# Experts with at most 64 rows: whole fp32 products in two column halves, weights in 8 KB runs, another order of the experts

## The chip, the cores and the metric

The program runs on one core of a Trainium2 chip, in one launch. Its time is the device time of that core in microseconds, the median of three runs. A separate execution was profiled; the rows below come from it.

## The reference, cut to what matters

The reference is one encoder block over 1024 + 512 tokens of width 1024: a projection, a pooling mixer, differential attention, an output projection, and a mixture of experts. The change touches the experts alone:

```python
hid = jax.nn.silu(xblk @ w_gate[e]) * (xblk @ w_up[e])    # 1024 -> 512, twice
y   = hid @ w_down[e]                                     # 512 -> 1024
# 32 experts; each token goes to 2 of them, its rows are gated and summed back
```

All of it is fp32. The three weights of an expert are 6 MB, so the 32 experts read about 200 MB whatever their rows are; a row (a token sent to an expert) costs a gather of 4 KB before and an adding scatter of 4 KB behind.

## The kernel before, in words

After attention and routing, `experts()` goes through a plan of 32 slots. The first two slots are fixed experts; the other 30 are filled at run time with the experts sorted by their number of rows, and each slot has a capacity in rows (`CAPS`, from 256 down to 32). `ORDER` says in which order the slots are worked off. Thirteen slots have a capacity of 64 or 32; this text calls them light, and the other seventeen plus the two fixed ones' rows heavy.

A slot is cut into blocks of at most 128 rows. For slot i, TensorE does gate(i), up(i) and then down(i-1), the down product of the slot before. Between the products stand transposes (L1109): those of the next slot's rows and those of the hidden values.

An fp32 product is not taken whole on this path. `split` (called from `use`, seven half-pieces ahead) writes a rounded copy `ew_hi` of the weights on ScalarE (L103) and the remainder `ew_lo` on VectorE (L107), both fp32r, and the rows get the same two parts. A block with more than 64 rows takes three fp32r products per 128 x 512 piece of weight (L111 to L113). A block of up to 64 rows has its high and low rows side by side as up to 128 columns of the stationary operand, and takes two (L1093, L1094); `both` adds the two halves of the result afterwards. In nine light slots, marked 4 in `NATIVE`, the down product is taken whole from the raw weights in fp32 (L1071), with the block's 64 or 32 columns as stationary operand; a whole product stands in the trace as two passes.

The raw weights come in pieces of 1 MB (`er_raw`, eight buffers), issued by SyncE in the order of their use (L1041), two pieces for each of gate, up and down. A buffer is free again when its split is done, or where the product is whole, when TensorE has read it. GpSimd issues the gathers (L1133, two slots ahead) and the adding scatters (L1179); each scatter waits for the one before it to land. The last two slots, 29 and 28, are not scattered before the end: their results are stacked and added by one matmul per half tile (L1207) to the sums that are read back from memory (`er_raw<-acc`, L1333, after the last scatter), and the final norm follows.

```python
NATIVE = (0,) * 17 + (4, 0, 4, 4, 4, 4, 0, 4, 0, 4, 4, 0, 4) + (0,) * STATIC
CAPS = (256,) * 2 + (224,) * 2 + (192,) + (160,) * 3 + (128,) * 4 + (96,) * 5 + (64,) * 9 + (32,) * 4 + (160, 128)
```

Of the kernel before, what the change touches and what calls it, by code (L numbers as in the profile page):

```python
# [10 lines left out]
F32 = mybir.dt.float32  # L11
F32R = mybir.dt.float32r
# [31 lines left out]
IDS = 4  # L44
AROWS = 64
PACE = (3, 1, 1, 1, 1, 1, 1, 0)
NATIVE = (0,) * 17 + (4, 0, 4, 4, 4, 4, 0, 4, 0, 4, 4, 0, 4) + (0,) * STATIC
DELAY = dict(out=1, hidden=1, silu=1, evac=1, turn_h=2, turn_x=4, end_h=3, stack=3)
ORDER = (11, 7, 26, 20, 23, 1, 24, 25, 14, 2, 21, 8, 3, 19, 18, 9, 4, 16, 5, 15, 0, 27, 22, 12, 13, 6, 17, 10, 29, 28)
CAPS = (256,) * 2 + (224,) * 2 + (192,) + (160,) * 3 + (128,) * 4 + (96,) * 5 + (64,) * 9 + (32,) * 4 + (160, 128)  # L50
VORDER = tuple(range(8, 12)) + tuple(range(8))
TGORDER = (2, 0, 1)
# [518 lines left out]
def layout(i):  # L571
    f = lambda n: np.asarray(i[n])
    a = {}
    x = np.concatenate([f("x_prompt")[0], f("x_sample")[0]], 0)
    a["x"] = x
    a["xT"] = x.T
    a["g_mix"] = f("g_mix")[0].reshape(8, 128).T
    a["pool_scale"] = f("pool_scale")[0].reshape(4, 128).T
    a["subln_g"] = f("subln_g")[0].reshape(128, 1)
    a["w_pool"] = f("w_pool")[0]  # L580
    for n in ("lambda_q1", "lambda_k1", "lambda_q2", "lambda_k2"):
        a[n] = f(n)[0]
    w = f("w_in")[0]
    pieces = []

    def piece(cols):
        n = cols.shape[1]
        k = cols.shape[0] // 128
        pieces.append(cols.reshape(k, 128, n).transpose(1, 0, 2).reshape(128, k * n))

    for g in range(2):
        piece(w[:, g * 256:(g + 1) * 256])
    for g in range(2):
        for o in (512, 1024):
# [12 lines left out]
    a["w_router"] = wr  # L607
    br = np.full((1, 40), -1e30, np.float32)
    br[0, :NE] = f("b_router_expert")[0]
    br[0, NE:NE + 4] = f("b_router_group")[0]  # L610
    a["b_router"] = br
    for n in ("w_gate", "w_up", "w_down"):
        a[n] = f(n)[0]
    return a


# [380 lines left out]
    nc.vector.scalar_tensor_tensor(K["ovs"], row[:1, :MAXOV], 128.0, st[:1], op0=OP.mult, op1=OP.add)  # L997


def natives(count):  # L1000

    return range(4) if count == 4 else range(1, 1 + count)


class Experts:
    def __init__(self, tc, A, S, K):
        self.tc, self.nc, self.A, self.S, self.K = tc, tc.nc, A, S, K
# [27 lines left out]
    def fetch(self, name, ev, i, queue=None):  # L1035
        n = D if name == "w_down" else FF
        k = 2048 // n
        raw = self.raw()
        w = self.A[name][ev:ev + 1] if isinstance(ev, int) else self.A[name][ds(ev, 1)]
        src = w.rearrange("o (k p) n -> p (o k) n", p=128)[:, i * k:(i + 1) * k]  # L1040
        (queue or self.nc.sync).dma_start(raw.rearrange("p (k n) -> p k n", k=k), src)  # L1041
        return raw, k

    def split(self, piece, h):
# [5 lines left out]
        split_lo(self.nc, lo, raw[:, s], hi)  # L1050
        return hi.rearrange("p (k n) -> p k n", k=k // 2), lo.rearrange("p (k n) -> p k n", k=k // 2)

    def ids(self, start, m, native=0, early=False):
# [3 lines left out]
        for p in range(0, 2 * m if m <= 64 else m, m):  # L1057
            nc.sync.dma_start(ix[p:p + m], src)
        return Block(self, m, ix, native, early, src)

    def proj(self, blocks, ps, w, i):
        for k in range(2):
            for b, p in zip(blocks, ps):
                b.mm(p, b.x, i * 2 + k, w[0][:, k], w[1][:, k], i + k == 0, i * 2 + k == 7)

    def down(self, blocks, ps, w, i):
        for b, (p0, p1) in zip(blocks, ps):
            for hf, p in enumerate((p0, p1)):
                s = slice(hf * 512, (hf + 1) * 512)
                if i in natives(b.native):  # L1070
                    self.nc.tensor.matmul(p[:b.m], lhsT=b.h[:, 0, i, :b.m].bitcast(F32), rhs=w[:, s], start=i == 0,  # L1071
                                          stop=i == 3)
                else:
                    b.mm(p, b.h, i, w[0][:, 0, s], w[1][:, 0, s], i == 0, i == 3)

    def bank(self):
        return self.PM([128, 512], F32, "m")
# [2 lines left out]
class Block:  # L1080


    def __init__(self, E, m, ix, native=0, early=False, src=None):
        self.native, self.early, self.src = native, early, src
        self.side = m <= 64
        self.E, self.nc, self.m, self.ix = E, E.nc, m, ix
        self.id = E.K["ident"]
        self.gate = ix[:, 1:2].bitcast(F32)

    def mm(self, p, x, k, wh, wl, first, last):  # L1090
        m = self.m
# [6 lines left out]
    def turn(self, out, src, n, pool=None):  # L1098

        nc, m = self.nc, self.m  # L1100
        per = min(4 if m > 64 else 8, n)

        def step(k0):
            p = []

            def fill():
                p.append((pool or self.E.PT)([128, per, m], F32, "t"))
                for k in range(per):
                    nc.tensor.transpose(p[0][:, k], src[:m, (k0 + k) * 128:(k0 + k + 1) * 128], self.id[:m, :m])  # L1109

            def empty():
                nat = natives(self.native) if n == 4 else range(0)
                if nat:
                    ks = slice(nat.start, nat.stop)
                    nc.scalar.activation(out[:, 0, ks, :m].bitcast(F32), p[0][:, ks], AF.Copy)
                for a, z in ((0, nat.start), (nat.stop, per)) if nat else ((0, per),):
                    if a == z:
                        continue
                    ks = slice(k0 + a, k0 + z)
                    hi = out[:, 0, ks, :m]  # L1120
                    lo = out[:, 0, ks, m:2 * m] if self.side else out[:, 1, ks, :m]
                    nc.scalar.activation(hi, p[0][:, a:z], AF.Copy)  # L1122
                    nc.vector.tensor_tensor(lo, p[0][:, a:z], hi.bitcast(F32), OP.subtract)  # L1123

            return fill, empty

        return [step(k0) for k0 in range(0, n, per)]
# [8 lines left out]
    def turn_x(self, pool=None):  # L1136
        if self.early:
            self.x = self.E.rows().bitcast(F32R).rearrange("p (o k m) -> p o k m", o=1, k=8)
        else:
            self.x = self.E.X([128, 2, 8, 128], F32R, "x", bufs=4)  # L1140
        return self.turn(self.x, self.xg, 8, pool)

    def turn_h(self):
        self.h = self.E.X([128, 2, 4, 128], F32R, "h", bufs=2)
        return self.turn(self.h, self.s, 4)

    def both(self, p, tag):
        nc, m = self.nc, self.m
        t = self.E.X([64, 512], F32, tag, bufs=1)[:m]
        nc.scalar.activation(t, p[m:2 * m], AF.Copy)  # L1150
        nc.vector.tensor_tensor(t, t, p[:m], OP.add)
        return t

# [13 lines left out]
    def weigh(self, ps):  # L1167
        nc, m = self.nc, self.m
        self.y = y = self.E.X([128, D], F32, "y")
        for hf, p in enumerate(ps):  # L1170
            d = y[:m, hf * 512:(hf + 1) * 512]
            if self.native == 4 or not self.side:
# [91 lines left out]
def experts(tc, A, S, K, RO, outs):  # L1264
    nc = tc.nc
    E = Experts(tc, A, S, K)
    with ExitStack() as ctx:
# [5 lines left out]
        def expert(i):  # L1273
# [4 lines left out]
                ev[i] = e  # L1278
            return ev[i]

        def ids(i):
            if i >= n:
                return
# [3 lines left out]
                o = AROWS  # L1287
            while o < cap:
                m = min(128, cap - o)
                bl.append(E.ids(expert(i) * ES + o, m, NATIVE[plan[i][0]]))  # L1290
                o += m
            blocks[i] = bl
            if i == n - 1:
# [51 lines left out]
        def split(k):  # L1345
            while at[1] < min(k, len(parts)):
                j = at[1] // 2
                fetch(j + 1)
                name, i, h, l = parts[at[1]]
                if name == "w_down" and h * 2 + l in natives(NATIVE[plan[i][0]]):  # L1350
                    pieces[parts[at[1]]] = raws[j][0][:, l * 1024:(l + 1) * 1024]
                else:
                    pieces[parts[at[1]]] = E.split(raws[j], l)
# [67 lines left out]
        for i in range(n + 1):  # L1421
# [24 lines left out]
            if i == n - 1:  # L1446
                after(DELAY["end_h"], lambda: turn(blocks[n - 1][0].turn_h()))
            if i:
                pd = [(E.bank(), E.bank()) for _ in blocks[i - 1]]
# [106 lines left out]
```

## Time and profile before

| what | us |
|---|---|
| median of 3 runs (1453.98 to 1455.87) | 1455.33 |
| the profiled execution | 1458.79 |
| its span, first to last instruction | 1456.5 |

The experts start at about 716 us of the span and their last product ends near 1401 us. Busy times are those of an engine, transfers are shown as the share of the 16 DMA engines, and a chain is the list of what released what, read from the end backwards. Matmul rows overlap their successors, so the distance between two starts, not the duration, is what one costs.

### The profile page before, as it was taken

To read this page: it belongs to the slowest core of one execution; us is meant where nothing else is said; L and a number is where in the kernel's file an instruction comes from. 1 tells how busy PE (TensorE), PEld (TensorE's weight loads), DVE (VectorE), ACT (ScalarE), POOL (GpSimd) and SP (SyncE) were. 2 spreads that over 40 slices of the span, in tenths; PEclk is the share of its full clock that TensorE was granted. 3 is DMA by queue.
4 is the path that set the end of the run, shared out by engine and by line. 5 is a ranking of instruction groups with operands and counts; after the bars stand their busy time and mean duration, and the time that the engine had idled before them with its cause. 6 is when DMAs were issued, how large, how long until landed. Compare 5 with 4: busy or idle time off the path is not lost.

```text
span 1456.5 us, 18022 instructions
## 1 busy us (share of the span) xinstructions
PE 1352.4 (93%) x5986; PEld 985.0 (68%) x5986; DVE 980.2 (67%) x1508; ACT 789.7 (54%) x1159; POOL 256.6 (18%) x376
## 2 busy tenths in 40 slices
PE   7899999987999999998599999999999999999970
PEld 5768888855667667876367757676767777667630
DVE  5486552085988637564677876877688786778774
ACT  6321112175887623221367776866587675777761
POOL 0000000003332210221211231322122221210132
PEclk9999999998999999999799999999999999999985
DMA  8535325066650057313699999999999997999874
GB/s 295 208 123 200 138 87 144 29 153 136 154 136 30 29 192 257 117 46 106 224 374 313 335 330 367 325 366 319 337 348 375 343 318 248 335 354 361 301 265 163
DMA packets 147694, 337.96 MB, mean 232 GB/s; under 512 B 17616, under 2 KB 25296, under 8 KB 147600
## 3 DMA queue, kind: packets, MB, share of 16 engines
q1 hardware_dynamic: 136688, 302.95, 60.0%
q0 software_dynamic: 9312, 29.65, 8.6%
q10 hardware_dynamic: 1600, 4.19, 0.8%
q8 instruction: 48, 0.79, 0.2%
q14 instruction: 46, 0.38, 0.1%
HBM read 282.69 MB, written 54.06 MB: 231 GB/s over the span
## 4 chain that ended last, share of the span: by engine, by line
PE 82%; DVE 6%; DMA 5%; ACT 2%; POOL 2%; issue 2%; SPq 0%; POOLq 0%; DVEq 0%; ACTq 0%
PE pm_m L111 9%; PE pm_m L113 9%; PE pm_m L112 9%; PE pm_m L1093 5%; PE pz_z L112 5%; PE pz_z L113 5%; PE pz_z L111 5%; PE pm_m L1094 5%; PE ps_sc L385 5%; PE po_o L443 4%; PE pm_m L1071 4%; PE pt_t L1109 3%; PE ph_h L112 2%; PE ph_h L111 2%; PE ph_h L113 2%; PE pt_t L430 2%
## 5 line engine op out<-in xcount | busy, mean ns | idle before, releaser
L107 DVE TENSOR_TENSOR ew_lo<-er_raw,ew_hi 128x1024 fp32r<-128x1024 f32 x348 | 413.1, 1218 | 113.3 <-ACT ew_hi L103 111.8
L103 ACT ACTIVATE ew_hi<-er_raw 128x1024 fp32r<-128x1024 f32 x348 | 354.9, 1052 | 55.5 <-PE pm_m L113 42.4
L111 PE MATMUL pm_m<-ew_hi,ex_x 128*128 128x512 f32 (+1 forms) x368 | 148.9, 405 | 0.2 <-ACT ex_x L1122 0.2
L113 PE MATMUL pm_m<-ew_hi,ex_x 128*128 128x512 f32 (+1 forms) x368 | 145.7, 396 | 0.2 <-DVE ex_x L1123 0.2
L112 PE MATMUL pm_m<-ew_lo,ex_x 128*128 128x512 f32 (+1 forms) x368 | 145.7, 396 | 0.0
L1179 POOL DMA_INDIRECT acc<-ex_y,ex_ix x40 | 90.4, 2260 | 251.3 <-ACT ex_y L1173 151.4
L111 PE MATMUL pz_z<-xT_hi,w_hi 128*128 128x512 f32 x288 | 114.8, 400 | 8.3 <-ACT xT_hi L152 8.3
L112 PE MATMUL pz_z<-xT_lo,w_hi 128*128 128x512 f32 x288 | 114.9, 399 | 0.0
L113 PE MATMUL pz_z<-xT_hi,w_lo 128*128 128x512 f32 x288 | 113.3, 393 | 0.0
L385 PE MATMUL ps_sc<-st_st 128*128 128x512 f32 x320 | 99.6, 452 | 11.5 <-ACT sm_e L404 5.6
L1093 PE MATMUL pm_m<-ew_hi,ex_x 128*128 128x512 f32 (+1 forms) x272 | 109.1, 401 | 0.0
L1094 PE MATMUL pm_m<-ew_lo,ex_x 128*128 128x512 f32 (+1 forms) x272 | 107.7, 396 | 0.1
L400 ACT ACTIVATE sm_e<-ps_sc,sb_m 128x1024 f32<-128x1024 f32 x64 | 70.8, 1111 | 45.6 <-PE pt_t L430 44.2
L389 DVE TENSOR_REDUCE sb_m<-ps_sc 128x1 f32<-128x1024 f32 x64 | 75.4, 1218 | 28.6 <-PE ps_sc L385 28.6
L385 PEld LDWEIGHTS ps_sc<-st_st 128*128 128x128 f32 x320 | 61.0, 198 | 47.7 <-issue 13.8
L111 PEld LDWEIGHTS pm_m<-ew_hi,ex_x 128*128 128x128 f32 (+1 forms) x368 | 66.0, 179 | 26.7 <-ACT ex_y L1173 3.3
L113 PEld LDWEIGHTS pm_m<-ew_hi,ex_x 128*128 128x128 f32 (+1 forms) x368 | 65.9, 179 | 20.8 <-DVE ex_x L1123 0.8
L443 PE MATMUL po_o<-wT_wT,v_V 128*128 128x512 f32 x160 | 78.8, 617 | 0.0
L112 PEld LDWEIGHTS pm_m<-ew_lo,ex_x 128*128 128x128 f32 (+1 forms) x368 | 66.1, 180 | 18.0
L111 PE MATMUL ph_h<-wo_woh,mx_mh 128*128 128x512 f32 x192 | 77.6, 405 | 0.1
L112 PE MATMUL ph_h<-wo_wol,mx_mh 128*128 128x512 f32 x192 | 77.1, 403 | 0.0
L113 PE MATMUL ph_h<-wo_woh,mx_ml 128*128 128x512 f32 x192 | 76.9, 400 | 0.0
(285 smaller groups left out, 2542.8 us busy)
## 6 DMA issues: line engine op xcount, KB each, us to landing
er_raw<-w_gate SPq DMA_DIRECT2D x64, 1024.0 KB, 10.0
er_raw<-w_up SPq DMA_DIRECT2D x62, 1024.0 KB, 10.5
er_raw<-w_down SPq DMA_DIRECT2D x62, 1024.0 KB, 10.9
st_st<-qk SPq DMA_DIRECT2D x48, 256.0 KB, 8.5
rw_raw<-w_in SPq DMA_DIRECT2D x16, 512.0 KB, 5.2
rw_raw<-xT SPq DMA_DIRECT2D x12, 512.0 KB, 5.6
x_x<-x SPq DMA_DIRECT2D x12, 512.0 KB, 5.5
qk<-rp_h SPq DMA_DIRECT2D x24, 256.0 KB, 2.0
```

What stands on the lines that cost most here:

```text
L103: nc.scalar.activation(hi, raw, AF.Copy)
L107: nc.vector.tensor_tensor(lo, raw, hi.bitcast(F32), OP.subtract)
L111: nc.tensor.matmul(out, lhsT=xh, rhs=wh, start=first, stop=False)
L112: nc.tensor.matmul(out, lhsT=xh, rhs=wl, start=False, stop=False)
L113: nc.tensor.matmul(out, lhsT=xl, rhs=wh, start=False, stop=last)
L385: nc.tensor.matmul(sc[:, b], lhsT=st[:, cc, 0, q0:q0 + 128], rhs=st[:, cc, i, k0:k0 + 512], start=i == 1, stop=i == 2)
L389: nc.vector.tensor_reduce(m[:, :1], sc, axis=AX.XY, op=OP.max, negate=True)
L400: nc.scalar.activation(e, sc, AF.Exp, bias=m[:, :1], accum_out=acc)
L443: nc.tensor.matmul(self.o, lhsT=V[:, self.t0 // 128 + kt, self.h * 128:(self.h + 1) * 128], rhs=self.wT[:, kt], start=kt == 0, stop=kt == ...
L1093: self.nc.tensor.matmul(p[:2 * m], lhsT=x[:, 0, k, :2 * m], rhs=wh, start=first, stop=False)
L1094: self.nc.tensor.matmul(p[:2 * m], lhsT=x[:, 0, k, :2 * m], rhs=wl, start=False, stop=last)
L1179: self.nc.gpsimd.indirect_dma_start(out=self.E.S["acc"], out_offset=bass.IndirectOffsetOnAxis(ap=self.ix[:self.m, 0:1], axis=0), in_=self. ...
```

## The change

Three things change together.

Blocks of slots with a capacity of at most 64 take every product whole, in fp32, straight from the raw weights: no `ew_hi`, no `ew_lo`, no low part of the rows. Two products share a PSUM bank: the even one writes partitions 0 to 63 of it (stationary columns 0 to 63 of the array), the odd one partitions 64 to 127. In gate and up the two are neighbouring pieces of the contraction, and `both` adds the halves; in down they are the two halves of the output. `NATIVE` goes.

The three weights are laid out on the host so that each 1 MB piece is one run of 8 KB per partition; before, a piece of gate or up came in runs of 2 KB and one of down in runs of 4 KB.

`ORDER` is another: lights stand singly or in twos between heavy slots. The last two slots stay; the one before them is slot 7 (160 rows), where slot 10 (128 rows) was.

```diff
-NATIVE = (0,) * 17 + (4, 0, 4, 4, 4, 4, 0, 4, 0, 4, 4, 0, 4) + (0,) * STATIC
+WHOLE = 64
-ORDER = (11, 7, 26, 20, 23, 1, 24, 25, 14, 2, 21, 8, 3, 19, 18, 9, 4, 16, 5, 15, 0, 27, 22, 12, 13, 6, 17, 10, 29, 28)
+ORDER = (17, 12, 0, 18, 26, 13, 1, 19, 20, 8, 2, 21, 27, 14, 3, 22, 23, 9, 4, 24, 15, 5, 25, 10, 6, 16, 11, 7, 29, 28)
...
     for n in ("w_gate", "w_up", "w_down"):
-        a[n] = f(n)[0]
+        w = f(n)[0]
+        k = w.shape[1] // 256
+        a[n] = w.reshape(NE, 2, k, 128, w.shape[2]).transpose(0, 1, 3, 2, 4).reshape(NE, 2, 128, 2048)
...
     def proj(self, blocks, ps, w, i):
+        if blocks[0].whole:
+            (b,), (p,) = blocks, ps
+            for k in range(2):
+                self.nc.tensor.matmul(p[b.at(k)], lhsT=b.x[:, i * 2 + k], rhs=w[:, k * 512:(k + 1) * 512],
+                                      start=i == 0, stop=i == 3)
+            return
...
     def down(self, blocks, ps, w, i):
...
-                if i in natives(b.native):
-                    self.nc.tensor.matmul(p[:b.m], lhsT=b.h[:, 0, i, :b.m].bitcast(F32), rhs=w[:, s], start=i == 0,
-                                          stop=i == 3)
+                if b.whole:
+                    self.nc.tensor.matmul(banks[0][b.at(hf)], lhsT=b.h[:, i], rhs=w[:, s], start=i == 0, stop=i == 3)
...
+    def at(self, k):
+
+        return slice(k * 64, k * 64 + self.m)
...
             def empty():
...
+                if self.whole:
+                    nc.scalar.activation(out[:, ks], p[0], AF.Copy)
+                    return
...
     def both(self, p, tag):
-        nc, m = self.nc, self.m
+        nc, m, o = self.nc, self.m, self.half
         t = self.E.X([64, 512], F32, tag, bufs=1)[:m]
-        nc.scalar.activation(t, p[m:2 * m], AF.Copy)
+        nc.scalar.activation(t, p[o:o + m], AF.Copy)
...
-                if name == "w_down" and h * 2 + l in natives(NATIVE[plan[i][0]]):
+                if whole(i):
                     pieces[parts[at[1]]] = raws[j][0][:, l * 1024:(l + 1) * 1024]
```

First place: TensorE at a light slot of 64 rows in the kernel before, part of up and the start of down. `ew_hi` and `ew_lo` are the split weights, `er_raw` raw ones, `ex_x` the rows, `ex_h` the hidden values, `pt4_t` a transpose, `pm_m` a PSUM bank.

```order
L1093 MATMUL pm_m_42_7152<-ew_hi_143_7125,ex_x_56_7052 128x512
L1094 MATMUL pm_m_42_7152<-ew_lo_144_7126,ex_x_56_7052 128x512
L1109 MATMUL pt4_t_21_7188<-k_ident_2_59,ex_xg_48_6960 128x128 x4
L1071 MATMUL pm_m_43_7197<-er_raw_29_6943,ex_h_61_7135 64x512
L1071 MATMUL pm_m_44_7198<-er_raw_29_6943,ex_h_61_7135 64x512
L1109 MATMUL pt4_t_22_7203<-k_ident_2_59,ex_xg_48_6960 128x128 x4
L1071 MATMUL pm_m_43_7197<-er_raw_29_6943,ex_h_61_7135 64x512
L1071 MATMUL pm_m_44_7198<-er_raw_29_6943,ex_h_61_7135 64x512
```

The same engine at a light slot of the changed kernel: all of gate and up, with the down product of the heavy slot before it behind.

```order
L1061 MATMUL pm_m_21_6309<-er_raw_7_5979,ex_x_20_6249 64x512 x4
L1119 MATMUL pt4_t_8_6344<-k_ident_2_59,ex_s_19_6221 128x128 x4
L1061 MATMUL pm_m_21_6309<-er_raw_8_5981,ex_x_20_6249 64x512 x4
L1061 MATMUL pm_m_22_6369<-er_raw_9_5997,ex_x_20_6249 64x512 x4
L1061 MATMUL pm_m_22_6369<-er_raw_10_6046,ex_x_20_6249 64x512 x4
L1119 MATMUL pt4_t_9_6400<-k_ident_2_59,exa_xg_3_6126 128x96 x4
L111 MATMUL pm_m_23_6409<-ew_hi_41_6349,ex_h_26_6343 128x512
```

Gate and up of a light slot were 32 fp32r products from split weights and are 16 whole ones from `er_raw`, two to a bank by turns; nothing of ScalarE or VectorE stands between the weights' landing and TensorE any more. Over the program there are 312 whole products in 67 unbroken runs where there were 72 in 20, and 120 fewer pairs of splits on ScalarE and VectorE.

Second place: TensorE at the end of the experts in the kernel before, down of slot 29 and the start of down of slot 28.

```order
L1071 MATMUL pm_m_171_11989<-er_raw_142_11770,ex_h_267_11934 32x512
L1071 MATMUL pm_m_172_11990<-er_raw_142_11770,ex_h_267_11934 32x512
L1109 MATMUL pt4_t_104_12008<-k_ident_2_59,ex_s_268_11956 128x32 x4
L1071 MATMUL pm_m_171_11989<-er_raw_142_11770,ex_h_267_11934 32x512
L1071 MATMUL pm_m_172_11990<-er_raw_142_11770,ex_h_267_11934 32x512
L1093 MATMUL pm_m_173_12017<-ew_hi_689_11967,ex_h_271_12007 64x512
```

And in the changed kernel, from the down product of slot 7 (second block, L1103 and L1104 are what L1093 and L1094 were) to the stacked matmul L1222.

```order
L1104 MATMUL pm_m_157_11149<-ew_lo_456_11119,ex_h_257_11077 64x512
L1061 MATMUL pm_m_158_11198<-er0_raw_47_10946,ex_x_262_11136 32x512 x4
L1119 MATMUL pt4_t_103_11218<-k_ident_2_59,ex_s_258_11113 128x32 x4
L1061 MATMUL pm_m_158_11198<-er0_raw_48_10985,ex_x_262_11136 32x512 x4
L1061 MATMUL pm_m_159_11230<-er_raw_139_11007,ex_x_262_11136 32x512 x4
L1061 MATMUL pm_m_159_11230<-er_raw_140_11043,ex_x_262_11136 32x512 x4
L1073 MATMUL pm_m_160_11248<-er_raw_141_11057,ex_h_267_11217 32x512 x4
L1073 MATMUL pm_m_160_11248<-er_raw_142_11072,ex_h_267_11217 32x512 x2
L1119 MATMUL pt4_t_104_11262<-k_ident_2_59,ex_s_268_11233 128x32 x4
L1073 MATMUL pm_m_160_11248<-er_raw_142_11072,ex_h_267_11217 32x512 x2
L1073 MATMUL pm_m_161_11270<-er_raw_143_11100,ex_h_271_11261 32x512 x4
L1222 MATMUL pm_m_162_11294<-ex_xg_264_11167,er0_raw_50_11165 128x512
```

Behind the last heavy down stand 32 whole products in three runs of 4, 18 and 10, with no split weights among them; before, 48 fp32r and 8 whole products stood there.

## Rows read from the trace of the kernel before

**Rows 1.** The page: busy us (share) of engines; slices of the span.

```profile
PE 1352.4 (93%) x5986; PEld 985.0 (68%) x5986; DVE 980.2 (67%) x1508; ACT 789.7 (54%) x1159; POOL 256.6 (18%) x376
...
PEclk9999999998999999999799999999999999999985
DMA  8535325066650057313699999999999997999874
```

**Rows 2.** The page: costliest groups, busy us, mean ns, idle before.

```profile
L107 DVE TENSOR_TENSOR ew_lo<-er_raw,ew_hi 128x1024 fp32r<-128x1024 f32 x348 | 413.1, 1218 | 113.3 <-ACT ew_hi L103 111.8
L103 ACT ACTIVATE ew_hi<-er_raw 128x1024 fp32r<-128x1024 f32 x348 | 354.9, 1052 | 55.5 <-PE pm_m L113 42.4
```

**Rows 3.** Stretches: us, busy of each engine, clock, DMA share, GB/s.

```profile
750.00:800.00 50.00, 50.00 (x236) 38.58 (x235) 39.81 (x43) 36.86 (x46) 8.70 (x7) 1.00 1.00 320
...
1300.00:1350.00 50.00, 50.00 (x233) 36.48 (x232) 39.81 (x44) 38.32 (x49) 8.86 (x5) 1.00 1.01 359
```

**Rows 4.** All waits of TensorE from 750 to 1376: total, times, longest.

```profile
PE pt_t L1109 <- DVE ex_x L1123: 0.2, 1, 0.2
```

**Rows 5.** The chain at two light slots: start, us, what.

```profile
837.04 0.24 PE pm_m L1093
837.28 0.24 PE pm_m L1094
837.51 0.23 PE pm_m L1093
837.75 0.23 PE pm_m L1094
...
840.49 6.98 PE pm_m L1071 x16
847.47 0.43 PE pm_m L1093
...
856.17 1.86 PE pm_m L1071 x4
858.03 0.59 PE pt_t L1109 x4
```

**Rows 6.** The chain at a third light slot.

```profile
1078.27 5.29 PE pm_m L1071 x12
```

**Rows 7.** Timeline near 857: start, us, engine, what.

```profile
856.58 1.02 PE L1071 MATMUL pm_m<-er_raw,ex_h 128*64 128x512 f32 x2
...
857.01 0.14 PEld L1071 LDWEIGHTS pm_m<-er_raw,ex_h 128*64 128x64 f32 x1 [0.29 <-issue]
```

**Rows 8.** Waits of SyncE's DMA queue from 750 to 1376.

```profile
SPq L1041 <- DVE ew_lo L107: 318.0, 116, 7.0
SPq L1041 <- PE pm_m L1071: 86.2, 16, 13.0
```

**Rows 9.** DMA queue from 1340.5 to 1349.5 (2 KB runs): packets, MB, share.

```profile
q1 hardware_dynamic: 1732, 3.45, 103.5%
```

**Rows 10.** DMA from 1382 to 1388 (4 KB runs).

```profile
DMA packets 642, 2.45 MB, mean 408 GB/s; under 512 B 45, under 2 KB 45, under 8 KB 642
...
q1 hardware_dynamic: 642, 2.45, 102.1%
```

**Rows 11.** The chain where the experts start.

```profile
719.52 9.11 DMA ex_xg<-hn,ex_ix
728.68 1.54 PE pt_t L1109 x8
```

**Rows 12.** DMA queues from 725 to 728.5, during that gather.

```profile
q0 software_dynamic: 131, 0.47, 47.1%
q1 hardware_dynamic: 139, 0.28, 30.2%
q10 hardware_dynamic: 141, 0.27, 26.8%
```

**Rows 13.** Timeline at the end of the experts.

```profile
1379.72 0.45 PE L1093 MATMUL pm_m<-ew_hi,ex_x 128*64 128x512 f32 x1
...
1383.84 1.96 POOL L1179 DMA_INDIRECT acc<-ex_y,ex_ix  x1 [4.20 <-ACT ex_y L1173]
...
1393.22 4.35 SPq L1333 DMA_DIRECT2D er_raw<-acc  x6
...
1403.51 0.47 PE L1207 MATMUL pm_m<-ex_xg,er_raw 128*128 128x512 f32 x1 [2.56 <-DVE ex_xg L107]
```

More of the change, by code (lines that the diff above doesn't have):

```diff
@@ L997, in schedule @@
     nc.vector.scalar_tensor_tensor(K["ovs"], row[:1, :MAXOV], 128.0, st[:1], op0=OP.mult, op1=OP.add)
-def natives(count):
-    return range(4) if count == 4 else range(1, 1 + count)
 class Experts:
@@ L1038, in fetch @@
         raw = self.raw()
-        w = self.A[name][ev:ev + 1] if isinstance(ev, int) else self.A[name][ds(ev, 1)]
-        src = w.rearrange("o (k p) n -> p (o k) n", p=128)[:, i * k:(i + 1) * k]
-        (queue or self.nc.sync).dma_start(raw.rearrange("p (k n) -> p k n", k=k), src)
+        w = self.A[name][ev:ev + 1, i] if isinstance(ev, int) else self.A[name][ds(ev, 1), i]
+        (queue or self.nc.sync).dma_start(raw, w.rearrange("o p n -> p (o n)"))
         return raw, k
@@ L1051, in split, with ids @@
         return hi.rearrange("p (k n) -> p k n", k=k // 2), lo.rearrange("p (k n) -> p k n", k=k // 2)
-    def ids(self, start, m, native=0, early=False):
+    def ids(self, start, m, whole=False, early=False):
         nc = self.nc
@@ L1056, in ids @@
         src = self.S["tab"][start:start + m] if isinstance(start, int) else self.S["tab"][ds(start, m)]
-        for p in range(0, 2 * m if m <= 64 else m, m):
+        for p in (0, 64) if whole else (0, m) if m <= 64 else (0,):
             nc.sync.dma_start(ix[p:p + m], src)
-        return Block(self, m, ix, native, early, src)
+        return Block(self, m, ix, whole, early, src)
     def proj(self, blocks, ps, w, i):
+        if blocks[0].whole:
[4 more added lines that the diff above has]
+            return
         for k in range(2):
@@ L1066, in down @@
     def down(self, blocks, ps, w, i):
-        for b, (p0, p1) in zip(blocks, ps):
-            for hf, p in enumerate((p0, p1)):
+        for b, banks in zip(blocks, ps):
+            for hf in range(2):
                 s = slice(hf * 512, (hf + 1) * 512)
-                if i in natives(b.native):
-                    self.nc.tensor.matmul(p[:b.m], lhsT=b.h[:, 0, i, :b.m].bitcast(F32), rhs=w[:, s], start=i == 0,
-                                          stop=i == 3)
+                if b.whole:
+                    self.nc.tensor.matmul(banks[0][b.at(hf)], lhsT=b.h[:, i], rhs=w[:, s], start=i == 0, stop=i == 3)
                 else:
-                    b.mm(p, b.h, i, w[0][:, 0, s], w[1][:, 0, s], i == 0, i == 3)
+                    b.mm(banks[hf], b.h, i, w[0][:, 0, s], w[1][:, 0, s], i == 0, i == 3)
     def bank(self):
@@ L1080, with __init__ @@
 class Block:
-    def __init__(self, E, m, ix, native=0, early=False, src=None):
-        self.native, self.early, self.src = native, early, src
+    def __init__(self, E, m, ix, whole=False, early=False, src=None):
+        self.whole, self.early, self.src = whole, early, src
         self.side = m <= 64
+        self.half = 64 if whole else m
         self.E, self.nc, self.m, self.ix = E, E.nc, m, ix
@@ L1111, in empty @@
             def empty():
[L1112 to L1123, printed above, removed]
+                ks = slice(k0, k0 + per)
+                if self.whole:
+                    nc.scalar.activation(out[:, ks], p[0], AF.Copy)
+                    return
+                hi = out[:, 0, ks, :m]
+                lo = out[:, 0, ks, m:2 * m] if self.side else out[:, 1, ks, :m]
+                nc.scalar.activation(hi, p[0], AF.Copy)
+                nc.vector.tensor_tensor(lo, p[0], hi.bitcast(F32), OP.subtract)
             return fill, empty
@@ L1139, in turn_x, with columns @@
         else:
-            self.x = self.E.X([128, 2, 8, 128], F32R, "x", bufs=4)
+            self.x = self.columns("x", 8, 4)
         return self.turn(self.x, self.xg, 8, pool)
     def turn_h(self):
-        self.h = self.E.X([128, 2, 4, 128], F32R, "h", bufs=2)
+        self.h = self.columns("h", 4, 2)
         return self.turn(self.h, self.s, 4)
+    def columns(self, tag, k, bufs):
+        t = self.E.X([128, 2, k, 128], F32R, tag, bufs=bufs)
+        return t[:, 0, :, :self.m].bitcast(F32) if self.whole else t
     def both(self, p, tag):
-        nc, m = self.nc, self.m
+        nc, m, o = self.nc, self.m, self.half
         t = self.E.X([64, 512], F32, tag, bufs=1)[:m]
-        nc.scalar.activation(t, p[m:2 * m], AF.Copy)
+        nc.scalar.activation(t, p[o:o + m], AF.Copy)
         nc.vector.tensor_tensor(t, t, p[:m], OP.add)
@@ L1169, in weigh @@
         self.y = y = self.E.X([128, D], F32, "y")
-        for hf, p in enumerate(ps):
+        for hf in range(2):
             d = y[:m, hf * 512:(hf + 1) * 512]
-            if self.native == 4 or not self.side:
+            if self.whole:
+                at = self.at(hf)
+                nc.scalar.activation(d, ps[0][at], AF.Copy, scale=self.gate[at])
+                continue
+            p = ps[hf]
+            if not self.side:
                 nc.scalar.activation(d, p[:m], AF.Copy, scale=self.gate[:m])
@@ L1279, in expert, with whole @@
             return ev[i]
+        def whole(i):
+            return CAPS[plan[i][0]] <= WHOLE
         def ids(i):
@@ L1289, in ids @@
                 m = min(128, cap - o)
-                bl.append(E.ids(expert(i) * ES + o, m, NATIVE[plan[i][0]]))
+                bl.append(E.ids(expert(i) * ES + o, m, whole(i)))
                 o += m
@@ L1448, in experts @@
             if i:
-                pd = [(E.bank(), E.bank()) for _ in blocks[i - 1]]
+                pd = [[E.bank() for _ in range(1 if b.whole else 2)] for b in blocks[i - 1]]
                 use(E.down, blocks[i - 1], pd, "w_down", i - 1)
```

## The prediction

> **What bounds the kernel now.** I read the page first: TensorE is busy for 93% of the span at nearly full clock, VectorE for 67%, ScalarE for 54%, and the DMA row shows eights and nines over the experts' half [rows 1]. So two things look full there, and the stretches tell which one binds: in each 50 us TensorE is busy for all 50.00 at clock 1.00, beside a DMA share of 1.00 or 1.01, while VectorE and ScalarE stay under 40 [rows 3]. The waits decide it. TensorE waited 0.2 us from 750 to 1376 [rows 4]; SyncE, which issues the weights, waited 318.0 us for splits to free a raw buffer and 86.2 us for TensorE to do so [rows 8]. Transfers run ahead and are held back by buffers; TensorE binds from 750 to the tail. What TensorE is spared is time saved, and what ScalarE, VectorE or a queue is spared is not.
>
> **Off the path: splits and layout.** 120 pairs of splits go: 120 x 1.218 = 146 us of VectorE and 120 x 1.052 = 126 us of ScalarE [rows 2]. They lay beside a TensorE without waits, so I put them at 0; below 0 is possible only in those 0.2 us. The 2 KB runs moved 3.45 MB in 9 us, 383 GB/s [rows 9], the 4 KB runs 408 GB/s [rows 10]. Gate and up are 2/3 of 200 MB, so at 408 or better some 134,000 x (1/383 - 1/408) = 21 us of transfer go, again at 0 behind the buffers. That cover is checked below.
>
> **TensorE up to the last heavy down, the light work.** Prices: a side product starts 0.235 us after the one before it [rows 5]. Of whole products, 16 rows of passes took 6.98 us and 4 took 1.86; 12 took 5.29 [rows 5, 6]. So eight passes more take 5.29 - 1.86 = 3.43 us, 0.429 a pass, and a run pays 1.86 - 4 x 0.429 = 0.144 once. A whole product is two passes, 0.858 us.
>
> Before, light slots hold there 12 x 32 + 3 x 16 = 432 side products (three downs of the split kind), 101.5 us; 8 whole downs of 8 products, 128 passes, 54.9; 18 runs x 0.144, 2.6. Sum 159.0 us.
>
> After, it is 280 whole products, 560 passes, in 64 runs. What these cost hangs on one thing that the trace doesn't show, since its passes all use the same 64 columns: how much of an odd product (columns 64 to 127) runs beside an even one. The bounds: nothing, 560 x 0.429 + 64 x 0.144 = 249.4 us; or everything, 280 x 0.429 + 9.2 = 129.3. I take a value between them, from the order. The queue holds both passes of product 1, both of product 2, and so on. Two passes on the same columns follow each other; the second pass of product 1 and the first of product 2 stand on different columns and can go together; the second of product 2 goes with the first of product 3. So N products in a run take N + 1 steps: (280 + 64) x 0.429 + 9.2 = 156.8 us, which is 2.2 us less than before. It lies nearest to the row of a side pair, 0.47 us for the same arithmetic.
>
> *A rule on that order.* The Trainium skill, "TensorE: Matmul & The Clock Gate", Part 3, "What overlaps and what doesn't", says that matmuls start and end strictly in program order; "TensorEngine Tiling (Array Packing)", Key Properties, says that different tiles of the array can load and multiply in parallel, and that changing the tiling mode drains the engine. Together they give the chain just worked out; the 0.144 us a run agrees with the drain, and no run here shows two tiles at once yet.
>
> Transposes between passes of whole products take 0.59 us [rows 5] where those between side products start 0.4 to 0.44 apart, by my estimate from the same stretch; some 46 more now stand so (+7 us), and some 36 more side products come right behind a whole run and take 0.43 instead of 0.235 (the row at 847.47 in [rows 5]) (that -7 us, since the run's price above already counts its end). I put the two at 0, with 4 us either way.
>
> **The start.** The first slot's gather is on the path: it takes 9.11 us and the transposes follow at once [rows 11]. Its queue q0 moved 131 packets while q1 moved 139 and q10 141 [rows 12]: the three take turns. 96 rows of 4 KB are six packets for each of 16 engines, so six turns in which two weight packets go first. A 2 KB packet takes 1.035 x 16 x 9 / 1732 = 0.086 us of an engine [rows 9], a 4 KB one some 0.164 (1.021 x 16 x 6 / 597, the small ones left out) [rows 10]; on that line an 8 KB one takes 0.32. Two longer packets a turn add 2 x 0.235 = 0.47 us, six turns 2.8 us. Bounds 0 and 2.8, since one of the queues may be empty for part of it; I take +2. Later gathers are issued two slots ahead and stay covered, at 0.
>
> **The tail.** From the last side product of the last heavy down, 1379.72, to the stacked matmul at 1403.51 it is 23.8 us [rows 13], with 48 side and 8 whole products between. After, 32 whole products stand there in three runs: 35 x 0.429 + 3 x 0.144 = 15.4, one pair of transposes 0.8, then what now lies between the last product and the stacked matmul, 3.0 (2.56 of it the wait in [rows 13]), and 1 for hand-overs between runs: 20.2, so -3.6. But the sums are read back only behind the last scatter. Before, the one scatter issued at 1383.84 had the readback at 1393.22, 9.4 us behind, and 10 us to spare until 1403.51 [rows 13]. Slot 7 has 160 rows, so two scatters, the second waiting for the first; a second one costs from 3.5 us (9.4 less the fixed part, my estimate) to 9.4, against a spare of 10 that the shorter tail cuts to about 6.5. Bounds for this -3.6 and +3; I take -3.3.
>
> **Cover of the transfers.** Raw buffers of light slots are now freed by TensorE alone. A light slot needs 6 x 1.05 MB / 408 GB/s = 15.4 us of transfer and, by the steps, 24 x 0.429 plus transposes and runs, 13 to 15 us of TensorE; a heavy one 15.4 plus its rows, and 17 to 37 us of TensorE. Two lights in a row fall behind by some 5 us; eight buffers of 1 MB are 20 us ahead. So 0. If that lead isn't there, 13 slots x 2.5 = 32 us.
>
> **Sum.** -2.2 + 2 - 3.3 = -3.5 against the profiled execution's 1458.79 (span 1456.5 and 2.3 around it). The median is 3.5 below that execution, so 1455.33 - 3.5, some **1452 us**.
>
> **Rivals.**
> - *Both halves fully side by side* (27.5 us less on the stretch than the chain): all products of the even columns overlap all of the odd. For it: a load of 64 columns, 0.14 us, runs while the pass before is still under way [rows 7], so passes are not closed units. Against it: the two passes of one product stand next to each other in the queue and in no row did two such passes overlap. About 1424.
> - *No overlap: slower.* The array takes one pass at a time, whatever its columns. For it: passes in every row start 0.429 apart [rows 5, 6] though half of the columns are idle. Then the stretch is 249.4, +90.4, the tail 64 + 3 steps, +9, the start +2: about 1557. It decides as soon as less than 75% of the odd products' 120 us is hidden (249.4 - 90.4 = 159.0).
> - *Loads that aren't hidden: slower.* The halves overlap but a half's load waits for the other half's pass, since both use the same 128 rows. At 0.14 us [rows 7] once per product 280 x 0.14 = +39, once per pair +20: 1472 to 1491. Against it: in rows 7 the load at 857.01 runs inside a pass that began at 856.58, on the same rows.
> - *Transfers late*: as priced above, 1452 + 32 = 1484; for it, the DMA share of 1.00 [rows 3], against it rows 8.
>
> *A rule against the change.* In rows 7 a load at 857.01 runs under the pass that began at 856.58. The Trainium skill, "TensorE: Matmul & The Clock Gate", Part 3, "What overlaps and what doesn't", says that a weight load overlaps a running matmul only when their row groups differ. Both column halves share all rows, so by the rule the unhidden loads above would be the result. The trace disagrees for passes on the same columns; no run shows it for different ones.
>
> **How the numbers follow.** A measurement of this kernel can't tell less than about 0.2%, 2.9 us. The chain, 0.43: by its own terms (4 for transposes, 3 for the tail, 2 for the start) 1446 to 1461, of which 0.24 is faster, 0.16 same and 0.03 slower. Fully side by side 0.22, faster. No overlap 0.16, unhidden loads 0.12, late transfers or a mishap of that size 0.07, all slower. So faster 0.46, same 0.16, slower 0.38. The range 1421 to 1490 leaves out no overlap and the edges of the others; the likeliest alone has 1446 to 1461.
>
> **What would show it.** Unbroken runs of whole products: four in a row are 5 steps, 2.15 us, by the chain; 1.7 fully side by side; 3.4 without overlap. Twelve are 5.6, 5.15 and 10.3. TensorE's waits from 750 to 1376 stay near 0, or else name `er_raw` and a DMA. SyncE's waits move from L107 to TensorE's L1061 and L1073. The opening gather takes about 11 us. VectorE's busy time falls by some 146 us and ScalarE's by 126 with no gain in the span by themselves. At the end the stacked matmul waits for VectorE again and not for the readback. The forecast is wrong if runs of whole products don't take N + 1 steps, or if TensorE waits for weights.

## The result, and the profile after

| | median us | runs | ratio to before, 95% interval |
|---|---|---|---|
| before | 1455.25 | 4 | |
| changed | 1434.05 | 4 (1429.75 to 1434.94) | 0.985 (0.9829 to 0.9871) |

The change takes 21 us off. The forecast was 1452 with a range of 1421 to 1490 and faster as the likelier side; the time is in the range, but 18 us under the forecast and outside what it gave the likeliest case (1446 to 1461). The profiled executions are 1458.79 and 1434.94, spans 1456.5 and 1432.7.

The page of the changed kernel, the rows that answer to [rows 1, 2]: busy us, share and instructions; slices of the span; the split's two groups (busy us, mean ns, idle before).

```profile
PE 1324.0 (92%) x5986; PEld 923.6 (64%) x5986; DVE 827.4 (58%) x1363; ACT 674.3 (47%) x1039; POOL 230.9 (16%) x376
...
PEclk9999999998999999999889999999999999999985
DMA  8635425057552047412497999898999999999674
...
L107 DVE TENSOR_TENSOR ew_lo<-er_raw,ew_hi 128x1024 fp32r<-128x1024 f32 x228 | 272.3, 1219 | 138.4 <-ACT ew_hi L103 135.1
L103 ACT ACTIVATE ew_hi<-er_raw 128x1024 fp32r<-128x1024 f32 x228 | 233.4, 1051 | 42.2 <-DMA er_raw<-w_gate 16.2
```

120 pairs of splits are gone, as foreseen: 141 us of VectorE's group, 122 us of ScalarE's; in all VectorE is busy for 153 us less and ScalarE for 115. TensorE has as many instructions as before, and it is busy for only 28 us less. Where its time went shows in the chain of the first light slot (start, us, what); 8 and 24 are passes, which is 4 and 12 products:

```profile
766.80 1.87 PE pm_m L1061 x8
768.67 0.59 PE pt_t L1119 x4
769.25 5.30 PE pm_m L1061 x24
```

24 passes take what 12 passes took before, 5.29 us [rows 6]. Four products are 1.87 us: 4 x 0.429 + 0.144, four steps and not the five (2.15 + 0.144) of my chain. The halves run fully side by side: in the single records all 624 passes start in pairs, the two of a pair at most 0.007 us apart, where no two whole passes of the kernel before start closer than 0.429 us. The weight loads don't stand in the way; in the timeline (start, us, engine, what) four loads of 64 columns, by the order of the code two for each half, lie within 0.20 us, while the first two passes have begun:

```profile
766.73 0.20 PEld L1061 LDWEIGHTS pm_m<-er_raw,ex_x 128*64 128x64 f32 x4 [0.38 <-issue]
```

Beside that gain stands a new wait. All waits of TensorE from 750 to 1376 (total us, times, longest), where [rows 4] had 0.2 us, and those of SyncE's queue, where [rows 8] had the splits first:

```profile
PE pt_t L1119 <- DVE ex_x L1129: 6.2, 6, 1.9
PE pm_m L1103 <- DVE ex_x L1129: 0.5, 1, 0.5
```

```profile
SPq L1037 <- PE pm_m L1061: 192.1, 36, 16.1
SPq L1037 <- DVE ew_lo L107: 132.2, 59, 6.4
SPq L1037 <- PE pm_m L1073: 72.4, 21, 9.6
```

I summed the distances between the starts of TensorE's matmuls by kind, from the first transposes of the experts to the stacked matmul, over the single records of both traces. A distance counts for the matmul that opens it, so a wait stands with the matmul ahead of it; the 6.2 us of waits of transposes are in the row of whole products:

| | before | changed | difference |
|---|---|---|---|
| side products | 168.5 | 48.9 | -119.5 |
| whole products, with the waits ahead of the transposes that follow them | 65.6 | 154.1 | +88.5 |
| other split products, and small ones | 396.0 | 398.7 | +2.7 |
| transposes, with the waits ahead of what follows them | 44.8 | 51.3 | +6.4 |
| sum | 674.8 | 652.9 | -22.0 |
| from the start of the span to the first transposes | 728.7 | 726.0 | -2.7 |
| from the stacked matmul to the end | 53.0 | 53.8 | +0.8 |

Little of the -2.7 can be the change's. The gather took 8.80 us against 9.11 [rows 11]; the other 2.4 were there before any expert, where the code is the same. Most of them fit the router's products, which ran while the granted clock was lower in the profile before, 0.91 of its upper level of 2.4 GHz over this stretch (20 us, first of the kernel before, then of the changed one; columns as in [rows 3]):

```profile
680.00:700.00 20.00, 17.38 (x86) 14.19 (x84) 11.23 (x35) 3.85 (x10) 0.00 (x0) 0.91 0.25 98
```

```profile
680.00:700.00 20.00, 15.11 (x82) 12.04 (x81) 12.41 (x48) 3.78 (x9) 0.00 (x0) 1.00 0.30 111
```

At the end, the stacked matmul starts 17.9 us after the first product behind the last heavy down (1361.03 to 1378.88) instead of 23.8 [rows 13], and the chain that ended last goes through the readback, not through it: the second scatter of slot 7, then the loads of the sums, whose landing the add waits for.

```profile
1370.35 3.97 DMA acc<-ex_y,ex_ix
...
1375.52 8.98 DMA er_raw<-acc
1384.49 0.60 DVE er_raw L1226
```

### The profile page after: what moved, and what is told of

It is laid out like the page before. It is cut to its first block, busy times and chain, and to the rows that moved or that the text cites. A ratio compares the mean times of both kernels' runs of the same rounds, so it can differ in the third digit from the quotient of the medians.

```text
span 1432.7 us, 17567 instructions
## 1 busy us (share of the span) xinstructions
PE 1324.0 (92%) x5986; PEld 923.6 (64%) x5986; DVE 827.4 (58%) x1363; ACT 674.3 (47%) x1039; POOL 230.9 (16%) x376
## 4 chain that ended last, share of the span: by engine, by line
PE 77%; DMA 9%; DVE 7%; ACT 2%; POOL 2%; issue 1%; SPq 0%; POOLq 0%; ACTq 0%; DVEq 0%
PE pm_m L111 8%; PE pm_m L113 8%; PE pm_m L112 8%; PE pm_m L1061 6%; PE pz_z L113 5%; PE pz_z L111 5%; PE pz_z L112 5%; PE ps_sc L385 4%; PE po_o L443 4%; DMA er_raw<-w_gate 4%; PE pt_t L1119 3%; PE ph_h L111 3%; PE ph_h L113 3%; PE ph_h L112 3%; PE pm_m L1073 2%; PE pt_t L430 2%
## 5 line engine op out<-in xcount | busy, mean ns | idle before, releaser
L107 DVE TENSOR_TENSOR ew_lo<-er_raw,ew_hi 128x1024 fp32r<-128x1024 f32 x228 | 272.3, 1219 | 138.4 <-ACT ew_hi L103 135.1
L103 ACT ACTIVATE ew_hi<-er_raw 128x1024 fp32r<-128x1024 f32 x228 | 233.4, 1051 | 42.2 <-DMA er_raw<-w_gate 16.2
L111 PE MATMUL pm_m<-ew_hi,ex_x 128*128 128x512 f32 (+1 forms) x368 | 149.8, 407 | 0.3 <-ACT ex_x L1128 0.3
L113 PE MATMUL pm_m<-ew_hi,ex_x 128*128 128x512 f32 (+1 forms) x368 | 146.1, 397 | 0.2 <-DVE ex_x L1129 0.2
L112 PE MATMUL pm_m<-ew_lo,ex_x 128*128 128x512 f32 (+1 forms) x368 | 145.7, 396 | 0.0
L1194 POOL DMA_INDIRECT acc<-ex_y,ex_ix x40 | 72.1, 1804 | 321.0 <-ACT ex_y L1188 145.9
L1061 PE MATMUL pm_m<-er_raw,ex_x 128*64 128x512 f32 (+1 forms) x416 | 96.3, 599 | 0.0
L112 PEld LDWEIGHTS pm_m<-ew_lo,ex_x 128*128 128x128 f32 (+1 forms) x368 | 66.4, 180 | 17.9
L111 PE MATMUL pm_m<-ew_hi,ex_h 128*128 128x512 f32 (+1 forms) x184 | 75.0, 408 | 0.0
## 6 DMA issues: line engine op xcount, KB each, us to landing
er_raw<-w_gate SPq DMA_DIRECT2D x64, 1024.0 KB, 12.6
```

Source lines behind the costliest of these rows:

```text
L103: nc.scalar.activation(hi, raw, AF.Copy)
L107: nc.vector.tensor_tensor(lo, raw, hi.bitcast(F32), OP.subtract)
L111: nc.tensor.matmul(out, lhsT=xh, rhs=wh, start=first, stop=False)
L112: nc.tensor.matmul(out, lhsT=xh, rhs=wl, start=False, stop=False)
L113: nc.tensor.matmul(out, lhsT=xl, rhs=wh, start=False, stop=last)
L1061: self.nc.tensor.matmul(p[b.at(k)], lhsT=b.x[:, i * 2 + k], rhs=w[:, k * 512:(k + 1) * 512], start=i == 0, stop=i == 3)
```

## Experiments

Each ratio is to runs of the kernel before on the same chip.

| kernel | whole products | 8 KB runs | new order | splits ahead | us | ratio, interval |
|---|---|---|---|---|---|---|
| only_layout | | x | | 7 | 1456.9 | 1.002 (1.000 to 1.004) |
| only_order | | | x | 7 | 1457.3 | 1.003 (1.001 to 1.005) |
| only_whole | x | | | 7 | 1456.9 | 1.002 (1.000 to 1.004) |
| old_order | x | x | | 7 | 1437.8 | 0.991 (0.988 to 0.994) |
| old_layout | x | | x | 7 | 1447.9 | 0.994 (0.992 to 0.996) |
| changed | x | x | x | 7 | 1434.1 | 0.985 (0.983 to 0.987) |
| ahead5 | x | x | x | 5 | 1424.1 | 0.979 (0.976 to 0.981) |
| ahead5_old | x | | x | 5 | 1427.1 | 0.980 (0.977 to 0.982) |
| raw9 (nine buffers) | x | x | x | 7 | 1429.6 | 0.982 (0.979 to 0.984) |
| raw9_old (nine buffers) | x | | x | 7 | 1437.7 | 0.985 (0.981 to 0.990) |

**The column halves.** In one_half all whole products stand on the same columns:

```diff
-    self.nc.tensor.matmul(p[b.at(k)], ..., start=i == 0, stop=i == 3)
+    self.nc.tensor.matmul(p[:b.m], ..., start=i + k == 0, stop=i * 2 + k == 7)
...
-    self.nc.tensor.matmul(banks[0][b.at(hf)], ...)
+    self.nc.tensor.matmul(banks[hf][:b.m], ...)
```

> The changed kernel, but all whole products on the same 64 columns (gate and up in one sum, down in two banks). Theory 1 (the two column halves run side by side, 0.429 us a pair of passes, and this is where the time went): 312 products then take 624 steps instead of 312, +134 us, less the 6 us of waits that the longer light slots cover: 1555 to 1570. Rival (the time went by the new order or the layout, the columns matter little): under 1455.

Measured 1556.9, ratio 1.069 (1.066 to 1.072): theory 1. In the chain at the same place eight passes take 3.58 us, which took 1.87 above:

```profile
765.72 3.58 PE pm_m L1061 x8
```

The 123 us are less than 134 partly because the 6.7 us of waits are gone: the trace has none of TensorE from 750 to 1500. The other 4 us stay unexplained.

**How far the queue is looked into.** The chain of my forecast rested on passes that start in the order in which the code issues them. grouped and grouped4 change that order:

```diff
+            if i % 2 == 0:
+                self.held = w
+                return
             for k in range(2):
-                self.nc.tensor.matmul(p[b.at(k)], lhsT=b.x[:, i * 2 + k], ...)
+                for j, v in ((i - 1, self.held), (i, w)):
+                    self.nc.tensor.matmul(p[b.at(k)], lhsT=b.x[:, j * 2 + k], ...)
...
```

(The same in down; grouped4 holds four half-pieces.)

> The changed kernel, products by twos: two on columns 0 to 63, then two on 64 to 127, instead of by turns. Theory 1a (each half of the columns has its own line, and the queue is looked into past a pass that waits): same as the changed kernel within 5 us, runs of four products 1.86 us. Theory 1b (only a pass and its neighbour in the queue go together): 6 steps instead of 4 for four products, 156 x 0.429 = +67 us, about 1500, a run of four 2.7 us.

> As grouped, but by fours: four products on columns 0 to 63, then four on 64 to 127, so that eight passes stand ahead of the first that could go beside them. Theory 1a with a look ahead of eight passes or more: within 5 us of the changed kernel, a run of eight 3.6 us. With a short look ahead, or theory 1b: up to 14 steps instead of 8, 39 x 6 x 0.429 = +100 us, about 1535.

Measured 1440.6, ratio 0.988 (0.985 to 0.992), and 1484.5, ratio 1.021 (1.017 to 1.025). For grouped that is theory 1a, with 1.87 us for a run of four, though the time is 6.5 us over the changed kernel and not within 5. grouped4 comes out between its two expectations: the look ahead is short, but costs less than I had. Twelve products of grouped still take twelve steps, and sixteen of grouped4 take 8.90 us, 20 steps and not 16 (start, us, what; first grouped, then grouped4):

```profile
771.43 5.35 PE pm_m L1065 x24
```

```profile
766.74 8.90 PE pm_m L1065 x32
```

Stretches of four steps (1.72 us) of that run of grouped4 show which steps stand alone. The columns are busy us of TensorE and of its loads, each with the number of passes or loads that touch the stretch, for these products alone; then clock, DMA share and GB/s:

```profile
766.60:768.32 1.72, 1.65 (x4) 0.60 (x5) 1.00 0.00 0
768.32:770.04 1.72, 1.72 (x9) 0.72 (x8) 1.00 0.72 79
770.04:771.76 1.72, 1.72 (x10) 0.72 (x8) 1.00 0.91 141
771.76:773.48 1.72, 1.72 (x10) 0.72 (x8) 1.00 0.71 281
773.48:775.20 1.72, 1.72 (x7) 0.41 (x3) 1.00 1.26 352
```

The first four of the eight passes of the one half run alone, then passes go in pairs, and the last four of the other half are alone again: 4 + 12 + 4 = 20 steps. So a pass of the free half starts while three earlier passes still wait (grouped, from its first pass on), and doesn't while four wait. In the single records the first two passes of that run of grouped start 0.013 us apart; in grouped4 the first pair is the fifth pass and one 0.006 us behind it. No record says which half a pass belongs to; that pairs are of different halves follows from one_half, which has none, and which of them was overtaken from the order of the code. By turns, as in the changed kernel, only one pass waits in front. As for the 6.5 us of grouped, in its profiled execution the row transposes waited 12.4 us instead of 6.2; that held products leave less time to the copies would fit, but no run separates it.

**The three parts of the change.**

> The kernel before with the 8 KB runs alone. My prediction's step (transfers run ahead there, TensorE waits 0.2 us): 1455 within 3. Rival (the 14 us that the layout is worth in the changed kernel are there in any order, as transfers are late behind the first gather or in the tail): 1441 to 1450.

> The kernel before with the new order of experts alone (nine native downs stay where their slots go). TensorE's work is the same as before, the tail longer by the second scatter of slot 7: 1455 to 1460. Rival (the order by itself is a gain): under 1450.

> The changed kernel with the old layout and the old order: whole products in column halves alone. Theory A (TensorE's 31 us of products are the whole gain, the rest costs or gives nothing): 1428 to 1436. Theory B (without the shorter transfers and the new order the light slots outrun the weights): 1445 to 1465, with 15 to 35 us of TensorE waits between 750 and 1376.

> The changed kernel with the order of experts of before (whole products and 8 KB runs stay). Theory A (the order matters little, TensorE's work is the same): 1431 to 1440. Theory B (the pace of the transfers counts now, and lights next to each other outrun them): TensorE waits for late weights, directly or behind ScalarE, for 10 to 25 us: 1442 to 1460.

> The changed kernel with the weights laid out as before (runs of 2 and 4 KB). Theory A (the layout lies off the path): within 3 us of the changed kernel. Theory B (light slots now outrun the transfers, so their pace counts: ScalarE's splits wait for weights at three places and TensorE's transposes behind them for 6 us): the 21 us of transfer that the 8 KB runs save come back in part, 1440 to 1455, with more waits of TensorE from 750 to 1376 than 6.7 us.

The edits put the lines of the other kernel in for one or two of the parts; old_order, for one:

```diff
-ORDER = (17, 12, 0, 18, 26, 13, 1, 19, 20, 8, 2, 21, 27, 14, 3, 22, 23, 9, 4, 24, 15, 5, 25, 10, 6, 16, 11, 7, 29, 28)
+ORDER = (11, 7, 26, 20, 23, 1, 24, 25, 14, 2, 21, 8, 3, 19, 18, 9, 4, 16, 5, 15, 0, 27, 22, 12, 13, 6, 17, 10, 29, 28)
```

None of the three parts gains anything alone. Layout and order alone are as I had them: where TensorE binds, a faster transfer is worth nothing. But the whole products alone are worth nothing either, although they save as much work as in the changed kernel: theory B. The old layout in the changed kernel is theory B too. Waits of TensorE from 750 to 1376 of only_whole, and two of its stretches:

```profile
PE pt_t L1118 <- DVE ex_x L1128: 24.7, 4, 9.7
PE pm_m L111 <- ACT ex_x L1127: 1.4, 1, 1.4
PE pm_m L113 <- DVE ex_x L1128: 0.6, 1, 0.6
```

```profile
850.00:900.00 50.00, 41.51 (x180) 24.87 (x180) 19.68 (x22) 20.64 (x28) 5.97 (x5) 0.90 0.92 307
900.00:950.00 50.00, 43.21 (x200) 24.65 (x200) 22.77 (x25) 25.78 (x36) 6.48 (x5) 0.93 1.05 368
```

It waits 26.7 us. In these stretches, in which TensorE waited 9.7 and 6.8 us at a time, the granted clock is 0.90 and 0.93 of its upper level of 2.4 GHz, and products run longer: the row "other split products, and small ones" of the table above would read 404.4 us, against 396.0 before. With the new order (old_layout) 15.6 us of waits are left, with the 8 KB runs (old_order) 12.6, with both 6.7. old_order is neither theory: A's range holds the median, B's waits are there, and two in five runs are above 1441. The order's share is about 4 us by the medians and 9 by the ratios, and no better settled than that; it was not run with splits five ahead.

**What TensorE waits for.** All of these waits but 1.4 us in only_whole name VectorE's copy of the next rows, which did nothing slow (0.68 us). One place in the changed kernel, the timelines of ScalarE, VectorE and TensorE (in brackets the idle time before, and what ended it):

```profile
871.13 2.01 ACT L103 ACTIVATE ew_hi<-er_raw 128x1024 fp32r<-128x1024 f32 x2 [3.14 <-DMA er_raw<-w_gate]
874.78 1.06 ACT L103 ACTIVATE ew_hi<-er_raw 128x1024 fp32r<-128x1024 f32 x1 [1.64 <-DMA er_raw<-w_gate]
875.74 0.58 ACT L1128 ACTIVATE ex_x<-pt_t 128x512 fp32r<-128x512 f32 x1
```

```profile
875.87 1.23 DVE L107 TENSOR_TENSOR ew_lo<-er_raw,ew_hi 128x1024 fp32r<-128x1024 f32 x1 [1.29 <-ACT ew_hi L103]
877.01 0.68 DVE L1129 TENSOR_TENSOR ex_x<-pt_t,ex_x 128x512 fp32r<-128x512 f32 x1
```

```profile
874.83 1.05 PE L1073 MATMUL pm_m<-er_raw,ex_h 128*32 128x512 f32 x4
877.75 0.66 PE L1119 MATMUL pt_t<-k_ident,ex_xg 128*128 128x128 f32 x4 [1.86 <-DVE ex_x L1129]
```

The rows transposed at 872.74 were ready to be copied at 873.3. In front of the copy in ScalarE's queue stood a split for the next heavy slot, whose weights landed at 874.78; the copy went at 875.74, VectorE's part at 877.01, behind VectorE's half of the same split, and TensorE got its transpose buffer back at 877.75. The weights weren't wanted by TensorE before 881.65. ahead5 issues the splits later, raw9 gives the transfers one buffer more:

```diff
-AHEAD = 7
+AHEAD = 5
```

```diff
-RAW, CUT = 8, 8
+RAW, CUT = 9, 8
...
-            self.x = self.columns("x", 8, 4)
+            self.x = self.columns("x", 8, 3)
```

> The changed kernel with splits issued five half-pieces ahead of their use instead of seven. Theory A (at three places a split that waits for late weights stands ahead of the copies of the next rows in ScalarE's queue, and TensorE's transposes wait behind those): the 6.2 us of waits of the row transposes fall under 3, 1426 to 1431. Theory B (the weights themselves are late, whoever stands in front of them): the wait moves to the heavy slot's first products, L111 for ew_hi or ew_lo, 1431 to 1437. Theory C (raw buffers are freed later and the transfers lose more of their lead): 1437 to 1450.

> The changed kernel with nine raw buffers of 1 MB instead of eight, paid for by one of the four buffers of turned rows. Theory A (what TensorE waits for is a lead of the transfers that is too short by a few us): one more buffer is 2.6 us of transfer, the 6.2 us of waits fall under 3, 1427 to 1432. Theory B (it is the rate of the transfers over a pair of slots, not the lead): 1432 to 1437, waits as before.

> The same nine buffers with the old layout (2 and 4 KB runs), against 1447.9 with eight. Theory A (lead): each of the four waits there (4.4, 3.2, 4.7, 3.4 us) is 2.6 us shorter, 1436 to 1441. Theory B (rate): 1445 to 1450.

> Five half-pieces ahead (as ahead5) with the old layout of the weights, against 1447.9 with seven and 1424.1 with five and the new layout. Theory A (the 14 us that the layout is worth are ScalarE's queue alone: a split that waits for weights holds back the copies behind it): no waits of TensorE's transposes left, 1424 to 1430. Theory B (2 and 4 KB runs are too slow for the light slots, whatever stands in ScalarE's queue): the wait moves to the heavy slot's first products, 1435 to 1446.

In all four it is theory A (ahead5 came out 2 us under its range). All waits of TensorE in ahead5 from 750 to 1376 are those of the stacked matmul in the tail:

```profile
PE pm_m L1222 <- DVE er_raw L1226: 3.0, 2, 2.0
PE pm_m L1222 <- DVE ex_xg L107: 2.9, 1, 2.9
```

At the same place a split for the heavy slot still waited for its weights (3.56 us), but ahead of the rows' transposes, and each copy now goes soon after them:

```profile
865.55 1.06 ACT L103 ACTIVATE ew_hi<-er_raw 128x1024 fp32r<-128x1024 f32 x1 [3.56 <-DMA er_raw<-w_gate]
867.37 0.60 ACT L1128 ACTIVATE ex_x<-pt_t 128x512 fp32r<-128x512 f32 x1 [0.76 <-PE pt_t L1119]
867.87 1.05 ACT L103 ACTIVATE ew_hi<-er_raw 128x1024 fp32r<-128x1024 f32 x1
868.94 0.60 ACT L1128 ACTIVATE ex_x<-pt_t 128x512 fp32r<-128x512 f32 x1
```

ahead5 is the fastest kernel of the study, 10 us under the changed one. ahead5_old shows what the layout was worth: 13.8 us with splits seven ahead, and 3 us with five, which the overlapping intervals don't tell from nothing. raw9's buffer takes the row waits from 6.2 to 0.6 us, raw9_old's from 15.6 to 2.9; in both a new wait of 3.8 comes up, of a transpose for VectorE's hidden values, and in raw9_old one of 1.4 for rows. So the weights were late by little, and a longer lead or a shorter queue in front of the copies removes the price either way.

## Why the prediction was right, and where it was wrong

The time is inside the range because the range had room for the rivals; the sum of -3.5 was wrong in its mechanism, and the likeliest case with it. Two errors partly cancelled: the light products were cheaper by some 27 us than the chain, and 9 us were given back around the waits behind late weights. Both signs by which I would have called the forecast wrong are there: runs don't take N + 1 steps, and TensorE waits, for copies that stand behind late weights and not with `er_raw` and a DMA named, as I had it.

- **What binds before: right.** Neither the layout nor the order alone moves the median by more than 0.3%.
- **The stretch, -2.2: wrong, by the step "N products in a run take N + 1 steps".** They go in N/2 pairs of two steps each, N steps in all, with no step for the end. The whole products of the stretch take 136.9 us in the changed kernel, some 7 of them at the waits, and 129.5 in ahead5, where I had 156.8 by the chain and 129.3 fully side by side; from the first transposes to the end of the last heavy down it is 651.0 us before and 635.0 after. I had let passes start in the queue's order only. The runs show that a pass of the other half goes past up to three waiting ones. The two rules of the Trainium skill that I had put together part here: "TensorEngine Tiling (Array Packing)", Key Properties (tiles load and multiply in parallel), agrees with the pairs of passes; "TensorE: Matmul & The Clock Gate", Part 3, "What overlaps and what doesn't" (matmuls in strict program order), is contradicted by grouped, where the pairs stand from the first pass of a run.
- **The rival "fully side by side", 1424, was the mechanism.** Of its 33 us on the stretch and in the tail 31 are there in ahead5, where the distance from first transposes to stacked matmul is 643.8 us: 25.1 of 29.7 on the stretch, and 5.9 instead of 3.3 in the tail. That its time is 1424.1 is luck in part, since the rival's 1424 has +2 for a start that wasn't there, and ahead5 isn't the kernel that I forecast. In the changed kernel 9 of these us are given back: 6.7 are the waits, and some of the rest goes with the granted clock, 0.93 of 2.4 GHz in the 25 us from 950, where TensorE waited.
- **"No overlap" and "loads that aren't hidden": fell.** The first is one_half, 1556.9 against my 1557 (which has +2 for the start, too). For the second I had +20 or +39 us; the 129.5 us of ahead5 against 129.3 without any such cost leave no room for it. The rule of the Trainium skill, "TensorE: Matmul & The Clock Gate", Part 3, "What overlaps and what doesn't", that a load overlaps only where row groups differ, has the trace against it for column halves too: four loads within 0.20 us, beside passes of 0.429 us on the same 128 rows. In [rows 7] the load at 857.01 starts together with the second of the two passes, and not only within the one from 856.58, as I read it; it runs under a pass either way.
- **The layout at 0, "hidden behind the buffers": right in the kernel before, wrong in the changed one**, where it is worth 13.8 us. I priced each part against the profile before; once the halves make light slots short, transfers no longer run ahead everywhere.
- **The cover of the transfers, 0: the failed step is "eight buffers are 20 us ahead".** The deficit was seen, its price not: I looked for TensorE waiting for weights, or 32 us in all. It waits 6.7 us, for copies of rows that stand in ScalarE's queue behind a split whose weights are late. I had counted the lead up to TensorE's use of the weights, but a split wants them seven half-pieces sooner: at 874.78 weights landed 6.9 us before TensorE's first product of that slot (881.65) and still too late for the split.
- **Transposes at 0, 4 either way: a little over the 4.** The +7 is there: transposes cost 6.4 us more, and 6.1 in ahead5, so it isn't the waits. The -7 against it is there only in part: in ahead5 the stretch falls 4.6 us short of the 29.7.
- **The start, +2: too high.** The gather took 8.80 us. Over the profiles TensorE's wait for it goes from 3.4 us (one_half) to 12.3 (only_layout), both with 8 KB runs, and from 3.5 to 9.8 with 2 KB runs: the packet's size doesn't show in it.
- **The tail, -3.3: half right.** The stacked matmul came 5.9 us sooner, where I had 3.6; the second scatter and the readback behind it took 0.8 back. The stacked matmul waited for VectorE, as I said, but the end hung on the readback, for which I had taken 0.3 us. (1379.72 is the first product behind the last heavy down and not the last of it; the distances are taken from there in both kernels.)

## What to carry to other kernels

Price the parts of a change together: what was hidden behind the engine that binds (here the transfers) was worth nothing until another part of the same change shortened that engine's work. An engine that binds can be held by a queue two engines away, so when a wait names a quick copy, look at what stood in front of that copy, and whether it was issued sooner than needed. And whole fp32 products with at most 64 columns of stationary operand can be issued on the two column halves by turns, which halved their time here.

## What the runs showed of the hardware that I had not expected

Whole fp32 passes on different column halves start out of the order in which the code issues them, past three waiting passes and not past four (grouped, grouped4). Two fp32 passes beside each other cost 0.429 us, the same as one: 24 passes in 5.30 us against 12 in 5.29.
